# Output projection of a hybrid SSD/GLA layer split around the last GLA heads, and its opening stage reordered

## The chip, the cores and the metric

The kernel runs on one core of one Trainium2 chip. It is one program with five engines (TensorE or PE, VectorE or DVE, ScalarE or ACT, GpSimd or POOL, SyncE or SP), each of which takes its own instructions in order, and with DMA queues that engines issue to. The metric is the device time of one execution in microseconds; three runs are shown of the kernel before.

## What is computed

Two layers of a backbone over 256 latent tokens and 256 context tokens, `D_MODEL` = 1024, all in float32. Only layer 0 and its entry are touched here:

```python
mod = silu(c) @ ada_w[layer] + ada_b[layer]      # 6 x 1024: sh1, sc1, g1, sh2, sc2, g2
h = rmsnorm(x, norm1_w) * (1 + sc1) + sh1
z, xbc, dt, q, k, v, lr, r = split(h @ w_in)      # one input projection
xbc = silu(conv(xbc)); y = ssd_scan(...); o = gla_scan(...)
y = rmsnorm((y + d_skip * x) * silu(z), groups=4) * ssd_norm_w
o = rmsnorm(o, per head) * gla_norm_w * silu(r)
x = x + g1 * (concat([y, o]) @ w_out)             # w_out: 2048 x 1024
x = x + g2 * (relu(norm2(x) @ w1) ** 2 @ w2)      # MLP
```

Both token streams (256 each) have their own modulation vector. Layer 1 (HGRN2 and S5) follows with the same frame.

## The kernel before, in words

Activations that feed a matmul are held transposed, as 8 tiles of 128 features x 512 tokens. Every float32 product is made of three matmuls of a split type: `hhi`/`hlo` are the high and low part of the activations, `whi`/`wlo` those of a weight tile, and `mm3` (line 101) adds hi x hi, hi x lo and lo x hi. A weight tile is loaded by `wtile` (line 211) into one of four `wraw` buffers on SyncE's queue, ScalarE makes `whi` of it and VectorE `wlo`. An output tile of 128 features is 8 k-tiles x 3 = 24 matmuls of 512 columns into one of four PSUM tiles `psd`. Smaller products use four PSUM tiles `pss`.

`ada_steps` (line 227) makes 2048 columns of the modulation as a generator: eight k-steps (two loads of 512 KB into `wraw` buffers, four matmuls that the trace lists as eight records), then a copy, then transposes into `mod`: ten steps. `step(ad)` runs it on by one. Group (0,1) holds g1, which the output projection needs; group (0,2) holds sc2 and g2, for the MLP's norm and its end.

The opening (up to line 829) loads 512 token rows, scales them by their inverse norm, transposes them to `xh`, makes the first 2048 columns of the modulation from `araw` loads in three chunks of k-tiles (0 to 3, 4 and 5, 6 and 7), applies them to get `h`, and uses each chunk for the first four tiles of the input projection. The rows without norm are transposed to `xT` too, which is written to a DRAM buffer `xd` from GpSimd's queue and read back for the residual.

Then come convolutions, the SSD chunks, and the GLA heads in four steps `t_` of two heads. `gla_in(t_)` projects q and k and makes the scan's factors and states in a chain of small operations over ScalarE, VectorE and PE; `gla_out(t_)` makes attention and outputs. As cover, the loop runs generators between them: `fill` (the z projection, one group of 256 columns a step, and at the end the SSD norm) by `ZN[t_]` steps and `ad` by `ADN[t_]`. After the loop, the output projection runs in two parts: 8 transposes of `xtm` (the SSD half), 8 tiles; then the same for `vtm` (the GLA half), of which the last four tiles are done by token halves with the next norm between.

The program is traced in this order, and a scheduler that simulates the engines' times then sets the order on each engine, earlier traced instructions first among those that it takes to be ready. Buffers of one ring are handed out in the order of the trace.

Of the kernel before, what the change touches and what calls it, by code (L numbers as in the profile page):

```python
# [26 lines left out]
CB = 4  # L27
NALT = 100
NID = 8
DTM = 11  # L30
NF = 4
AR = 12
ZN = 3, 1, 2, 2
ADN = 0, 6, 11, 0
WA = 0, 1
QP = -2, 1, 2, 5
VP = -2, -1, 0, -1
GP = -1, 0, 4, 6
# [3 lines left out]
def emit(tc, A, out):  # L42
# [63 lines left out]
    def tr(o, i, rows=P):  # L106
        PE.transpose(o, i, ident[:rows, :rows])  # L107
# [646 lines left out]
    xn = tl(sp, [P, 4, DM], "xn")  # L754
    xh = tl(sp, [P, 8, T], "xh")
    ss = tl(sp, [P, 4], "ss")
    for b in range(2):
        for c in (2 * b, 2 * b + 1):
            S.activation(out=xn[:, c], in_=xt[:, c], func=AF.Square, accum_out=ss[:, c:c + 1])
        s2_ = ss[:, 2 * b:2 * b + 2]  # L760
        act(s2_, s2_, AF.Ln, scale=1.0 / DM, bias=eps)
        act(s2_, s2_, AF.Exp, scale=-0.5)
        for c in (2 * b, 2 * b + 1):
            ts(V, xn[:, c], xt[:, c], ss[:, c:c + 1], MUL)
    for k in range(8):
        ps = ps_s()
        for c in range(4):
            tr(ps[:, c * P:(c + 1) * P], xn[:, c, k * P:(k + 1) * P])
        if k % 2:
            V.tensor_copy(xh[:, k], ps)  # L770
        else:
            act(xh[:, k], ps, AF.Copy)
    h = tuple(tl(hp, [P, 8, T], n_, F32R) for n_ in ("hhi", "hlo"))
    scl = tl(cp, [P, 8, 2], "ms01")
    W0 = A["ssd_gla_w_in"][0]
    W1i = A["hgrn_s5_w_in"][0]
    order = (8, 9, 10, 11, 12, 13, 14, 15, 0, 1, 2, 3, 4, 5, 6, 7)
    first = {}
    for k0, nk in ((0, 4), (4, 2), (6, 2)):
        ps = ps_s()  # L780
        ks, n = slice(k0, k0 + nk), nk * P
        for kk in range(0, 8, 4 // nk):

            raw = tl(sp, [P, 4 // nk, 2, n], "araw", bufs=AR)
            for j in range(2):
                Q.dma_start(out=raw[:, :, j], in_=A["ada_w"][0, kk * P:(kk + 4 // nk) * P, j * DM + k0 * P:j * DM + k0 * P + n].rearrange(
                    "(k p) c -> p k c", p=P))
            for k in range(4 // nk):
                for g in range(4):
                    PE.matmul(ps[32 * g:32 * g + 32, :n // 2], lhsT=cs[:, kk + k],  # L790
                              rhs=raw[:, k, g // 2, n // 2 * (g % 2):n // 2 * (g % 2) + n // 2],
                              start=(kk + k == 0), stop=(kk + k == 7), skip_group_check=True, tile_position=(0, 32 * g))
        wq = [wtile(W0, kk, 2, 1024 + P * order[0], NF * P) for kk in range(k0, k0 + nk, 2)]
        if k0 == 0:
            small_t(ra, vA, P)
        sb = tl(sp, [P, 256], "adasb")
        act(sb[:, :n // 2], ps[:, :n // 2], AF.Copy)
        p2 = ps_s()
        nb = nk // 2
        for b in range(nb):  # L800
            tr(p2[:, b * P:(b + 1) * P], sb[:, b * P:(b + 1) * P])
        dst = mod[0][:, 0:16].rearrange("p (j k) s -> p j k s", j=2)[:, :, ks].rearrange("p j (h b) s -> p j h b s", h=2)
        src = p2[:, :nb * P].rearrange("p (b j h r) -> p j h b r", b=nb, j=2, h=2)[:, :, :, :, 0:2]
        bias = vA[:, 0:16].rearrange("p (j k) -> p j k", j=2)[:, :, ks].rearrange("p j (h b) -> p j h b", h=2)
        for s in range(2):
            for j in range(2):
                tt(V, dst[:, j, :, :, s], src[:, j, :, :, s], bias[:, j], ADD)
        mod_scale(scl, 0, 1, ks)
        for k in range(k0, k0 + nk):
            for s in (1, 0):  # L810
                sc_, sh_ = scl[:, k, s:s + 1], mod[0][:, k, s:s + 1]
                act(h[0][:, k, HALF[s]], xh[:, k, HALF[s]], AF.Identity, scale=sc_, bias=sh_)
                ts(V, xh[:, k, HALF[s]], xh[:, k, HALF[s]], sc_, MUL, sh_, ADD)
            tt(V, h[1][:, k], xh[:, k], h[0][:, k], SUB)
        for i, m in enumerate(order[:NF]):
            if k0 == 0:
                first[m] = ps_d()
            c_ = slice(P * i, P * i + P)
            for kk in range(k0, k0 + nk):
                w = [w_[:, kk % 2, c_] for w_ in wq[(kk - k0) // 2]]  # L820
                mm3(first[m], w, (h[0][:, kk], h[1][:, kk]), kk == 0, kk == 7)
        for k in range(k0, k0 + nk):
            ps = ps_s()
            for c in range(4):
                tr(ps[:, c * P:(c + 1) * P], xt[:, c, k * P:(k + 1) * P])
            act(xT[:, k], ps, AF.Copy)
    small_t(rb, vB, 104)
    small_t(rc, vC, P)
    st.close()
# [16 lines left out]
    def dt_proj():  # L846

        raw = tl(wp, [P, 8, P], "wraw", bufs=RAW)
        V.memset(raw, 0.0)
        for i, c0 in enumerate((3072, 3088, 5152, 5168)):  # L850
            Q.dma_start(out=raw[:, :, 32 * i:32 * i + 16], in_=W0[:, c0:c0 + 16].rearrange("(k p) c -> p k c", p=P))
        w = wsplit(raw, 8, P)
        ps = ps_d()
        gemm_f(ps, w, ktiles(h))
        act(dlr, ps, AF.Copy)
# [469 lines left out]
            lin_out(g2, pmask, units, put)  # L1325

    scr[0] = lambda: tl(g2, [P, T], "ge1", bufs=2)
    cur = gla_in(0, gla_w(0))
    wn = gla_w(1)
    for t_ in range(4):  # L1330
        step(fill, ZN[t_])
        nxt = gla_in(t_ + 1, wn) if t_ < 3 else None
        wn = gla_w(t_ + 2) if t_ < 2 else None
        step(ad, ADN[t_])
        if t_ == 3:
            drain(fill)
            step(ad, max(0, 10 - adn[0]))
        gla_out(t_, cur)
        cur = nxt
    gla.close()  # L1340


    lo_eng[:] = [V]
    WO = A["ssd_gla_w_out"][0]
    mgs = ExitStack()
    mg = pool("mixg", stack=mgs, side="right")
    scr[0] = lambda: tl(mg, [P, T], "adasb")
    for part, src in enumerate((xtm, vtm)):
        if part == 0:
            mx = [tl(hp, [P, 8, T], n, F32R) for n in ("hhi", "hlo")]  # L1350
        else:
            mx = [tl(mg, [P, 8, T], n, F32R) for n in ("mgh", "mgl")]
        for f in range(8):
            ps = ps_s()
            for c in range(4):
                tr(ps[:, c * P:(c + 1) * P], src[:, c, f * P:(f + 1) * P])
            nw = vB[:, 16 + f:17 + f] if part == 0 else vB[:, 96:97]
            act(mx[0][:, f], ps, AF.Copy, scale=nw)
            stt(V, mx[1][:, f], ps, nw, mx[0][:, f], MUL, SUB)
        if part == 0:  # L1360
            xT = tl(xp, [P, 8, T], "xtm")
            S.dma_start(out=xT, in_=xd.rearrange("k p t -> p k t"))
        def add_out(m):
            def put(s, ps):
                a = HALF[s]
                stt(V, xT[:, m, a], ps[:, a], mod[0][:, 16 + m, s:s + 1], xT[:, m, a], MUL, ADD)
            return put

        nf = 8 if part == 0 else 4
        for m in range(nf):  # L1370
            step(ad, WA[part])
            w = wtile(WO, 8 * part, 8, m * P, P)
            ps = ps_d()
            gemm_f(ps, w, ktiles(mx))
            for s in (1, 0):
                add_out(m)(s, ps)
# [346 lines left out]
```

## Time and profile before

| | |
|---|---|
| median of 3 runs | 1479.78 us (1475.62 to 1483.78) |
| the profiled execution | 1482.16 us, span 1480.4 us |
| PE busy | 1426.6 us, 96% |
| DVE, ACT, POOL busy | 942.2, 688.3, 303.0 us |
| mean granted clock of PE | 0.973 |
| HBM read, written | 206.39 MB, 14.46 MB |

An engine's busy time counts its instructions' spans, so a PE at half clock is as busy as at full clock; the granted clock has to be read beside it (1.00 is 2.4 GHz, 0.50 is 1.2 GHz). The page's slices show the clock at or near 9 (that is 0.9 or more) throughout, except for two slices of 8 and 5 some way into the span. The chain that ended last lies on PE for 78% of the span.

### The profile page before, as it was taken

Reading aid. Unit: us, or ns where it says so; the run is one execution under the profiler, and the core shown is the slowest. Engines: PE = TensorE matmul, PEld = TensorE weight load, DVE = VectorE, ACT = ScalarE, POOL = GpSimd, SP = SyncE. Lnnn points to the kernel's source line nnn. Section 1 sums busy time; section 2 is a strip of 40 time slices with the busy share of each in tenths; the row PEclk is TensorE's granted clock in tenths of the full one; section 3 lists DMA queues with packets and bytes.
Section 4 is the critical chain, followed back from the end, with each engine's and each line's share of the span. In section 5 each row is a group of like instructions: output and inputs, shape, how many; then the busy total and the mean of one; then the engine's idle time right before and its main releaser. Section 6 shows DMA issues by size and latency. Waiting matters only on the chain.

```text
span 1480.4 us, 24457 instructions
## 1 busy us (share of the span) xinstructions
PE 1426.6 (96%) x9662; PEld 1222.3 (83%) x9662; DVE 942.2 (64%) x1596; ACT 688.3 (46%) x1316; POOL 303.0 (20%) x340
## 2 busy tenths in 40 slices
PE   6999999999979999999999999999999999899998
PEld 4788998878746889877777777799988888899998
DVE  4698678876753455854563743374886988655543
ACT  5565545375532234531322422353286786555532
POOL 3000000000000003098077861122500000044210
PEclk9999999999985999999999999999999999999999
DMA  9733444421275433466467656649835332566762
GB/s 333 185 92 85 126 122 118 125 58 58 86 240 160 138 103 105 121 179 197 143 187 218 192 169 186 192 165 202 194 114 157 103 106 66 157 186 170 206 179 86
DMA packets 291151, 222.45 MB, mean 150 GB/s; under 512 B 22902, under 2 KB 270124, under 8 KB 291036
## 3 DMA queue, kind: packets, MB, share of 16 engines
q1 hardware_dynamic: 252752, 182.75, 42.5%
q0 software_dynamic: 6144, 22.05, 4.9%
q10 hardware_dynamic: 32140, 16.09, 4.4%
q8 instruction: 76, 1.25, 0.4%
q14 instruction: 39, 0.32, 0.1%
HBM read 206.39 MB, written 14.46 MB: 149 GB/s over the span
## 4 chain that ended last, share of the span: by engine, by line
PE 78%; DVE 8%; DMA 8%; ACT 4%; issue 2%; ACTq 0%; SPq 0%; DVEq 0%
PE psd L99 65%; PE pss L99 6%; DMA R<-acd 3%; PE pss L237 3%; PE pss L107 2%; DMA araw<-in_ada_w_dram 2%; DVE wlo L87 1%; DMA wraw<-in_ada_w_dram 1%; ACT hL L80 1%; DVE xtm L87 1%; ACT whi L80 1%; PE pss L652 1%; DMA U<-ud 0%; DMA ud<-s5r 0%; ACT R L80 0%
## 5 line engine op out<-in xcount | busy, mean ns | idle before, releaser
L87 DVE TENSOR_TENSOR wlo<-wraw,whi 128x1024 fp32r<-128x1024 f32 (+1 forms) x250 | 323.6, 1298 | 206.7 <-ACT whi L80 205.0
L80 ACT ACTIVATE whi<-wraw 128x1024 fp32r<-128x1024 f32 (+1 forms) x250 | 260.6, 1045 | 351.7 <-DMA wraw<-in_mlp_w_dram 170.7
L99 PE MATMUL psd<-hlo,whi 128*128 128x512 f32 (+1 forms) x1112 | 381.6, 345 | 1.3 <-DVE hlo L87 1.3
L99 PE MATMUL psd<-hhi,whi 128*128 128x512 f32 (+1 forms) x1112 | 378.5, 348 | 3.6 <-ACT hhi L80 3.6
L99 PE MATMUL psd<-hhi,wlo 128*128 128x512 f32 (+1 forms) x1112 | 380.8, 344 | 0.6 <-DVE wlo L87 0.6
L99 PEld LDWEIGHTS psd<-hhi,whi 128*128 128x128 f32 x1112 | 209.5, 191 | 36.0 <-ACT hhi L80 4.2
L99 PEld LDWEIGHTS psd<-hlo,whi 128*128 128x128 f32 x1112 | 211.3, 190 | 25.2 <-DVE hlo L87 2.3
L99 PEld LDWEIGHTS psd<-hhi,wlo 128*128 128x128 f32 x1112 | 211.3, 190 | 25.1 <-DVE wlo L87 1.0
L99 PE MATMUL psd<-wlo,hhi 128*128 128x256 f32 x576 | 165.5, 288 | 2.8 <-DVE wlo L87 2.8
L99 PE MATMUL psd<-whi,hlo 128*128 128x256 f32 x576 | 164.8, 286 | 0.0
L99 PE MATMUL psd<-whi,hhi 128*128 128x256 f32 x576 | 164.4, 287 | 0.0
L99 PEld LDWEIGHTS psd<-wlo,hhi 128*128 128x128 f32 x576 | 111.1, 193 | 4.7 <-DVE wlo L87 3.0
L99 PEld LDWEIGHTS psd<-whi,hhi 128*128 128x128 f32 x576 | 110.8, 193 | 2.7 <-issue 1.3
L99 PEld LDWEIGHTS psd<-whi,hlo 128*128 128x128 f32 x576 | 111.1, 193 | 0.6 <-issue 0.2
L99 PE MATMUL psd<-hidh,whi 128*128 128x512 f32 (+1 forms) x288 | 107.7, 375 | 0.0
L99 PE MATMUL psd<-hidl,whi 128*128 128x512 f32 (+1 forms) x288 | 105.6, 367 | 0.0
L99 PE MATMUL psd<-hidh,wlo 128*128 128x512 f32 (+1 forms) x288 | 105.5, 366 | 0.0
L87 POOL TENSOR_TENSOR nsa<-nsa,nsq 128x256 f32<-128x256 f32 x28 | 26.1, 934 | 370.1 <-ACT nsq L80 369.8
L96 DVE SCALAR_TENSOR_TENSOR xtm<-psd,mod,xtm 128x256 f32<-128x256 f32 x96 | 42.2, 476 | 66.6 <-PE psd L99 59.2
L99 PE MATMUL psd<-hl,whi 128*128 128x256 f32 x256 | 72.9, 285 | 0.0
L99 PE MATMUL psd<-hh,wlo 128*128 128x256 f32 x256 | 72.9, 285 | 0.0
L99 PE MATMUL psd<-hh,whi 128*128 128x256 f32 x256 | 72.4, 283 | 0.0
(448 smaller groups left out, 2447.4 us busy)
## 6 DMA issues: line engine op xcount, KB each, us to landing
wraw<-in_mlp_w_dram SPq DMA_DIRECT2D x128, 512.0 KB, 4.2
wraw<-in_ada_w_dram SPq DMA_DIRECT2D x80, 512.0 KB, 3.8
wraw<-in_ssd_gla_w_in_dram SPq DMA_DIRECT2D x48, 512.0 KB, 4.2
wraw<-in_hgrn_s_w_in_dram SPq DMA_DIRECT2D x43, 512.0 KB, 4.2
araw<-in_ada_w_dram SPq DMA_DIRECT2D x32, 256.0 KB, 7.8
R<-acd ACTq DMA_DIRECT2D x32, 256.0 KB, 3.9
wraw<-in_ssd_gla_w_out_dram SPq DMA_DIRECT2D x16, 512.0 KB, 4.6
wraw<-in_hgrn_s_w_out_dram SPq DMA_DIRECT2D x12, 384.0 KB, 3.4
```

Of the source, the lines that this page charges most:

```text
L80: ins = S.activation(out=out_, in_=in_, func=func, scale=scale, bias=bias)
L87: eng.tensor_tensor(out=o, in0=a, in1=b, op=op)
L96: eng.scalar_tensor_tensor(out=o, in0=a, scalar=s, in1=b, op0=op0, op1=op1)
L99: PE.matmul(o, lhsT=l, rhs=r, start=start, stop=stop, skip_group_check=True)
L107: PE.transpose(o, i, ident[:rows, :rows])
L237: ins = PE.matmul(ps[32 * gg:32 * gg + 32], lhsT=cs[:, k], rhs=raws[gg // 2][:, gg % 2 * T:gg % 2 * T + T], start=(k == 0), stop=(k == 7), ...
L652: PE.matmul(ps[64 * t2:64 * t2 + 64, 64 * a:64 * a + 64], lhsT=W1[i][:, a0 + a, 64 * t2:64 * t2 + 64], rhs=U[:, 2 * (a0 + a) + t2], start= ...
```

## The change

The output projection's loop is cut in two. A generator `ssd_out` holds the transposes of `xtm`, the load of `xT` and the eight tiles of the SSD half, with one step of `ad` ahead of each tile. The GLA loop runs it by `SN` = 0, 0, 5, 4 steps: five (the transposes and four tiles) behind `gla_out(2)` and four behind `gla_out(3)`. The GLA half stays behind the loop. `ADN` changes from 0, 6, 11, 0 to 0, 6, 4, 0, so group (0,1) is completed ahead of `gla_out(2)`, and the k-steps of (0,2) go with the tiles. `ZN` changes from 3, 1, 2, 2 to 2, 1, 1, 1, and what is left of `fill` (the last steps, with the norm) is run ahead of `gla_out(2)` instead of `gla_out(3)`.

In the opening, the 512 raw rows are transposed to `xT` right after they are loaded (VectorE copies them out of PSUM, ScalarE copies `xh`), the chain from the modulation's matmuls to `h` gets priority in the scheduler, and the first four tiles are fed k-tile by k-tile instead of tile by tile. The small dt projection is made after convolution tile 13 instead of 11, and its buffer is cleared by GpSimd instead of VectorE.

```diff
-DTM = 11
+DTM = 13
-ZN = 3, 1, 2, 2
-ADN = 0, 6, 11, 0
-WA = 0, 1
+ZN = 2, 1, 1, 1
+ADN = 0, 6, 4, 0
+SN = 0, 0, 5, 4
...
+    def turned(src, b, put):
+        for k in range(0, 8, 2):
+            ps = ps_s()
+            for i in range(4):
+                tr(ps[:, i * P:(i + 1) * P], src[:, 2 * b + i % 2, (k + i // 2) * P:(k + i // 2 + 1) * P])
+            put((slice(None), slice(k, k + 2), slice(256 * b, 256 * b + 256)), ps.rearrange("p (k t) -> p k t", k=2))
...
-    for k in range(8):
-        ps = ps_s()
-        for c in range(4):
-            tr(ps[:, c * P:(c + 1) * P], xn[:, c, k * P:(k + 1) * P])
-        if k % 2:
-            V.tensor_copy(xh[:, k], ps)
-        else:
-            act(xh[:, k], ps, AF.Copy)
+        turned(xt, b, lambda at, ps: V.tensor_copy(xT[at], ps))
+        turned(xn, b, lambda at, ps: act(xh[at], ps, AF.Copy))
...
+        with tc.high_priority():
             sb = tl(sp, [P, 256], "adasb")
...
-        for i, m in enumerate(order[:NF]):
-            if k0 == 0:
-                first[m] = ps_d()
-            c_ = slice(P * i, P * i + P)
-            for kk in range(k0, k0 + nk):
+        if k0 == 0:
+            first = {m: ps_d() for m in order[:NF]}
+        for kk in range(k0, k0 + nk):
+            for i, m in enumerate(order[:NF]):
...
                 mm3(first[m], w, (h[0][:, kk], h[1][:, kk]), kk == 0, kk == 7)
-        for k in range(k0, k0 + nk):
-            ps = ps_s()
-            for c in range(4):
-                tr(ps[:, c * P:(c + 1) * P], xt[:, c, k * P:(k + 1) * P])
-            act(xT[:, k], ps, AF.Copy)
...
-        V.memset(raw, 0.0)
+        G.memset(raw, 0.0)
...
+    def out_tile(mx, part, m):
+        w = wtile(WO, 8 * part, 8, m * P, P)
+        ps = ps_d()
+        gemm_f(ps, w, ktiles(mx))
+        for s in (1, 0):
+            add_out(m)(s, ps)
+
+    def ssd_out():
+        mx = [tl(hp, [P, 8, T], n, F32R) for n in ("hhi", "hlo")]
+        turned_mix(mx, xtm, 0)
+        res["x"] = tl(xp, [P, 8, T], "xtm")
+        S.dma_start(out=res["x"], in_=xd.rearrange("k p t -> p k t"))
+        yield
+        for m in range(8):
+            step(ad)
+            out_tile(mx, 0, m)
+            yield
...
+    so = ssd_out()
     for t_ in range(4):
         step(fill, ZN[t_])
         nxt = gla_in(t_ + 1, wn) if t_ < 3 else None
         wn = gla_w(t_ + 2) if t_ < 2 else None
         step(ad, ADN[t_])
-        if t_ == 3:
+        if t_ == 2:
             drain(fill)
-            step(ad, max(0, 10 - adn[0]))
+            step(ad, 10 - adn[0])
         gla_out(t_, cur)
+        step(so, SN[t_])
         cur = nxt
     gla.close()
```

`turned_mix` holds the eight groups of transposes with their scaling into `hhi`/`hlo`, as they stood in the loop before.

## Rows read from the trace of the kernel before

**Rows 1.** Stretches: length, busy us (instructions) by engine, granted clock, DMA share, GB/s.
```profile
0.00:31.70 31.70, 17.12 (x168) 12.37 (x168) 13.12 (x34) 16.44 (x34) 12.43 (x28) 1.00 0.96 322
300.00:310.00 10.00, 7.21 (x48) 7.00 (x48) 9.42 (x13) 8.40 (x20) 0.00 (x0) 0.83 0.03 5
398.60:440.00 41.40, 31.97 (x278) 16.71 (x279) 25.94 (x45) 16.25 (x51) 0.00 (x0) 0.92 0.73 246
440.00:486.00 46.00, 46.00 (x205) 29.38 (x206) 17.85 (x26) 10.43 (x42) 0.00 (x0) 0.51 0.55 168
745.00:830.00 85.00, 85.00 (x443) 62.97 (x443) 44.33 (x44) 23.45 (x31) 67.62 (x55) 1.00 0.69 200
```

**Rows 2.** Waits of PE, 398.6 to 486 us: total, times, longest.
```profile
PE pss L237 <- DMA wraw<-in_ada_w_dram: 8.2, 5, 3.2
```

**Rows 3.** Timeline of PE, 400 to 452 us: start, length, instructions, idle before.
```profile
400.49 0.97 PE L99 MATMUL pss<-g0qt,g0kt 64*64 64x128 f32 x15
...
402.95 1.06 PE L99 MATMUL pss<-g0qt,g0kt 64*64 64x128 f32 x16 [0.25 <-DVE pm L1193]
405.01 1.06 PE L237 MATMUL pss<-wraw,cs 128*32 128x512 f32 x8 [1.01 <-DMA wraw<-in_ada_w_dram]
406.01 1.09 PE L99 MATMUL pss<-g1qt,g1kt 64*64 64x64 f32 x16
...
410.81 1.06 PE L237 MATMUL pss<-wraw,cs 128*32 128x512 f32 x8
...
422.53 1.06 PE L237 MATMUL pss<-wraw,cs 128*32 128x512 f32 x8 [3.20 <-DMA wraw<-in_ada_w_dram]
...
426.66 1.93 PE L237 MATMUL pss<-wraw,cs 128*32 128x512 f32 x8 [2.23 <-DMA wraw<-in_ada_w_dram]
...
451.69 1.97 PE L99 MATMUL pss<-g0qt,g0kt 64*64 64x128 f32 x16
```

**Rows 4.** Timeline of SyncE's queue, 355 to 560 us.
```profile
370.38 88.87 SPq L233 DMA_DIRECT2D wraw<-in_ada_w_dram  x28
```

**Rows 5.** The chain that ended last: start, length, what, how many.
```profile
290.18 6.95 PE psd L99 x58
...
512.86 20.89 PE psd L99 x92
```

**Rows 6.** DMA issues, 396 to 486 us: count, size, median us to landing.
```profile
wraw<-in_ada_w_dram SPq DMA_DIRECT2D x26, 512.0 KB, 5.3
wraw<-in_ssd_gla_w_out_dram SPq DMA_DIRECT2D x8, 512.0 KB, 4.2
```

**Rows 7.** DMA issues, 745 to 830 us (MLP of layer 0).
```profile
wraw<-in_mlp_w_dram SPq DMA_DIRECT2D x14, 512.0 KB, 5.5
wraw<-in_ada_w_dram SPq DMA_DIRECT2D x12, 512.0 KB, 3.6
```

**Rows 8.** Timeline of PE, opening.
```profile
30.63 1.17 PE L790 MATMUL pss<-araw,cs 128*32 128x128 f32 x16 [0.33 <-DMA araw<-in_ada_w_dram]
31.72 1.19 PE L99 MATMUL psd<-hhi,whi 128*128 128x512 f32 x4
...
51.19 1.94 PE L790 MATMUL pss<-araw,cs 128*32 128x128 f32 x58
...
53.66 1.04 PE L107 MATMUL pss<-ident,xt 128*128 128x128 f32 x8
...
56.41 1.20 PE L99 MATMUL psd<-hhi,whi 128*128 128x512 f32 x4 [1.51 <-ACT hhi L80]
```

**Rows 9.** Timeline of ScalarE, opening.
```profile
26.77 2.06 ACT L80 ACTIVATE xT<-pss 128x512 f32<-128x512 f32 x4
28.69 4.04 ACT L80 ACTIVATE hhi<-xh,mod,ms 128x256 fp32r<-128x256 f32 x8
```

**Rows 10.** Timeline of GpSimd: first and last of the four writes of `xT`.
```profile
28.15 0.77 POOL L887 DMA_DIRECT2D xd<-xT  x1 [12.69 <-ACT xT L80]
...
57.63 0.71 POOL L887 DMA_DIRECT2D xd<-xT  x1 [17.40 <-DMA wraw<-in_ssd_gla_w_in_dram]
```

More of the change, by code (lines that the diff above doesn't have):

```diff
@@ L777, in emit @@
     order = (8, 9, 10, 11, 12, 13, 14, 15, 0, 1, 2, 3, 4, 5, 6, 7)
-    first = {}
     for k0, nk in ((0, 4), (4, 2), (6, 2)):
@@ L795, in emit @@
             small_t(ra, vA, P)
[L796 to L808, printed above, removed]
-        for k in range(k0, k0 + nk):
[L810 to L814, printed above, removed]
@@ L815, in emit @@
-        for i, m in enumerate(order[:NF]):
-            if k0 == 0:
-                first[m] = ps_d()
-            c_ = slice(P * i, P * i + P)
-            for kk in range(k0, k0 + nk):
-                w = [w_[:, kk % 2, c_] for w_ in wq[(kk - k0) // 2]]
-                mm3(first[m], w, (h[0][:, kk], h[1][:, kk]), kk == 0, kk == 7)
-        for k in range(k0, k0 + nk):
-            ps = ps_s()
-            for c in range(4):
-                tr(ps[:, c * P:(c + 1) * P], xt[:, c, k * P:(k + 1) * P])
-            act(xT[:, k], ps, AF.Copy)
+        with tc.high_priority():
+            sb = tl(sp, [P, 256], "adasb")
+            act(sb[:, :n // 2], ps[:, :n // 2], AF.Copy)
+            p2 = ps_s()
+            nb = nk // 2
+            for b in range(nb):
+                tr(p2[:, b * P:(b + 1) * P], sb[:, b * P:(b + 1) * P])
+            dst = mod[0][:, 0:16].rearrange("p (j k) s -> p j k s", j=2)[:, :, ks].rearrange("p j (h b) s -> p j h b s", h=2)
+            src = p2[:, :nb * P].rearrange("p (b j h r) -> p j h b r", b=nb, j=2, h=2)[:, :, :, :, 0:2]
+            bias = vA[:, 0:16].rearrange("p (j k) -> p j k", j=2)[:, :, ks].rearrange("p j (h b) -> p j h b", h=2)
+            for s in range(2):
+                for j in range(2):
+                    tt(V, dst[:, j, :, :, s], src[:, j, :, :, s], bias[:, j], ADD)
+            mod_scale(scl, 0, 1, ks)
+            for k in range(k0, k0 + nk):
+                for s in (1, 0):
+                    sc_, sh_ = scl[:, k, s:s + 1], mod[0][:, k, s:s + 1]
+                    act(h[0][:, k, HALF[s]], xh[:, k, HALF[s]], AF.Identity, scale=sc_, bias=sh_)
+                    ts(V, xh[:, k, HALF[s]], xh[:, k, HALF[s]], sc_, MUL, sh_, ADD)
+                tt(V, h[1][:, k], xh[:, k], h[0][:, k], SUB)
@@ L827, in emit @@
+        if k0 == 0:
+            first = {m: ps_d() for m in order[:NF]}
+        for kk in range(k0, k0 + nk):
+            for i, m in enumerate(order[:NF]):
+                w = [w_[:, kk % 2, P * i:P * i + P] for w_ in wq[(kk - k0) // 2]]
+                mm3(first[m], w, (h[0][:, kk], h[1][:, kk]), kk == 0, kk == 7)
     small_t(rb, vB, 104)
@@ L1327, in emit, with turned_mix @@
     scr[0] = lambda: tl(g2, [P, T], "ge1", bufs=2)
[L1328 to L1334, printed above, removed]
-        if t_ == 3:
-            drain(fill)
-            step(ad, max(0, 10 - adn[0]))
[L1338 to L1343, printed above, removed]
-    WO = A["ssd_gla_w_out"][0]
[L1345 to L1352, printed above, removed]
+    WO = A["ssd_gla_w_out"][0]
+    res = {}
+    def turned_mix(mx, src, part):
         for f in range(8):
@@ L1359, in emit, with add_out, put @@
             stt(V, mx[1][:, f], ps, nw, mx[0][:, f], MUL, SUB)
[L1360 to L1376, printed above, removed]
+    def add_out(m):
+        def put(s, ps):
+            a = HALF[s]
+            x_ = res["x"][:, m, a]
+            stt(V, x_, ps[:, a], mod[0][:, 16 + m, s:s + 1], x_, MUL, ADD)
+        return put
+    def out_tile(mx, part, m):
+        w = wtile(WO, 8 * part, 8, m * P, P)
+        ps = ps_d()
+        gemm_f(ps, w, ktiles(mx))
+        for s in (1, 0):
+            add_out(m)(s, ps)
[9 more added lines that the diff above has]
+            yield
+    cur = gla_in(0, gla_w(0))
+    wn = gla_w(1)
+    so = ssd_out()
+    for t_ in range(4):
+        step(fill, ZN[t_])
+        nxt = gla_in(t_ + 1, wn) if t_ < 3 else None
+        wn = gla_w(t_ + 2) if t_ < 2 else None
+        step(ad, ADN[t_])
+        if t_ == 2:
+            drain(fill)
+            step(ad, 10 - adn[0])
+        gla_out(t_, cur)
+        step(so, SN[t_])
+        cur = nxt
+    gla.close()
+    lo_eng[:] = [V]
+    mgs = ExitStack()
+    mg = pool("mixg", stack=mgs, side="right")
+    scr[0] = lambda: tl(mg, [P, T], "adasb")
+    mx = [tl(mg, [P, 8, T], n, F32R) for n in ("mgh", "mgl")]
+    turned_mix(mx, vtm, 1)
+    xT = res["x"]
+    for m in range(4):
+        step(ad)
+        out_tile(mx, 1, m)
     drain(ad)
```

## The prediction

> **What bounds the kernel now.** I read the page first: TensorE (PE) is busy for 96% of the span, so only time in which it waits, or in which it runs at its lower clock, can be won. The table of stretches says where that is [rows 1]. From 398.6 to 440.0 us PE is busy for 31.97 of 41.4 us. From 440.0 to 486.0 us it is busy all the time, but at a granted clock of 0.51, which is the 1.2 GHz level instead of 2.4: 22.5 of these 46 us are lost although no idle time shows. Outside this stretch only short holes are left, as the 2.8 us of 300 to 310 us.
>
> The list of waits says what PE waited for there: the loads of `ada_w`, 8.2 us in five waits [rows 2]. The timeline shows the mechanism [rows 3]. PE runs the small matmuls of `gla_out` and, between them, one k-step of `ada_steps` after another (eight records, 1.06 us at full clock). It takes its instructions in order, so a k-step whose two loads have not landed stops all of it: 1.01 us at 405.01, 3.20 at 422.53, 2.23 at 426.66. After these holes the clock is down, and the attention block that took 1.06 us at 402.95 takes 1.97 at 451.69. The queue of SyncE shows the cause of the holes: from 370.38 us it needs 88.87 us for 28 loads, 3.17 us each, through the four `wraw` buffers [rows 4]. Dense work is not there to stand in between: the tiles of the output projection come after all of it, and their eighth ends at 512.86 + 20.89 = 533.8 us in the chain that ended last [rows 5].
>
> **The late stretch, from the eighth k-step on.** The steps of (0,1) are finished at 426.66 + 1.93 = 428.6 us [rows 3], and the change keeps all eight of them ahead of `gla_out(2)`. From there to 533.8 us the kernel now takes 105.2 us. The same work after the change, at full clock:
> - 8 tiles of the SSD half x 24 matmuls x 0.227 us (20.89 us for 92 [rows 5]) = 43.6 us.
> - 8 k-steps x 1.06 us = 8.5 us. Now seven of them stand in this stretch and the last behind it, so 1.1 us comes back later.
> - `gla_out(2)` and `gla_out(3)`, two heads each. One pair at full clock: the attention blocks from 400.49 to 402.95 less a wait of 0.25 (2.2 us), then 1.06 and 1.09; the first head's outputs from there to 410.81 (3.7), and as much for the second: 11.75 us [rows 3]. Two pairs: 23.5 us.
> - 32 transposes of `xtm` at 0.13 us (eight `xt` transposes of the same form take 1.04 us [rows 8]) = 4.1 us.
>
> Sum 79.7 us, so 25.5 us less, and with the k-step behind it 26.6. What remains of the loss must be taken off. Loads: 24 of them in 79.7 us is one per 3.32 us. The MLP of layer 0 ran 26 in 85 us, 3.27 us each, with PE busy throughout at full clock [rows 1, 7], so this pace is carried; I charge 2 us for the uneven mixture (two loads for a k-step, one for a tile), between 0 and the pace at which all is serial (rival 4). Clock: the dense tiles stand between the two pairs of heads, but an isolated pair may still run low; I charge 4 us, between 0 and 23.5 (both pairs at 1.2 GHz). That leaves -20.6 us.
>
> **Before 428.6 us.** The fourth group of z moves from ahead of `gla_in(2)` to behind it: 96 matmuls at 0.12 us (6.95 us for 58 [rows 5]) = 11.5 us of dense work that can now stand in the 6.4 us of waits between 405 and 427 [rows 3]. Its two weight loads queue behind twelve `ada_w` loads in SyncE's queue, so it may itself come late. I take half, -3.2 us (0 to -6.4). In return `t_` = 0 has one group of z less as cover, where 2.8 us of hole are today [rows 1]: 0, at worst +2.8. Norm, transposes of `xtm`, and their scaling on ScalarE and VectorE now fall among the chains of heads 4 to 7, but both engines are busy for less than two thirds there (25.94 and 16.25 of 41.4 us [rows 1]). The load of `xT` from `xd` moves ahead by some 60 us on ScalarE's queue, where it can hold up what is behind it only until the last of the 32 transposes is done; the 4 us above cover that. Dropping one accumulation order for another in `first` changes no count of matmuls.
>
> **The opening.** PE reaches its first projection matmul at 31.72 us, behind `ada_w` matmuls that waited for their load (0.33 us at 30.63). From there to the end of the first four tiles it is in work except for gaps of the small chain: the last `araw` matmul ends at 53.13 and the next projection matmul starts at 56.41, 3.3 us, in which eight `xt` transposes are the filler [rows 8]. The change takes the `xt` transposes to the first 20 us, when PE is waiting anyway: two groups of eight stand behind 31.72 today, but one of them only fills that gap, so 0.8 us. The chain gets priority: ScalarE's one `xT` copy in that gap goes, 0.6 us. At the start, ScalarE runs four `xT` copies (2.06 us) before the first `hhi` at 28.69 [rows 9], and VectorE's memset of the dt weights goes to GpSimd; of these 2.06 us I take 0.6, because the first matmul also stands behind that load. Sum -2.0, at best -3.5. The dt weights, issued after the m = 13 tile instead of m = 11, are wanted only by the dt stage behind all convolutions, so moving them is taken as 0.
>
> Against it: `xT` is complete some 10 us earlier, and GpSimd, idle then, writes it to `xd` at once. The four writes of 512 KB are issued from 28.15 to 57.63 us today [rows 10]. The DMA engines are full all that time: share 0.96, 322 GB/s [rows 1]. All 2.1 MB ahead of the loads of chunk two would cost them 2.1 MB / 322 GB/s = 6.5 us, and 3.3 if half of them fall ahead of those loads already today. I take 0 for the forecast, since PE has 48 matmuls (10.9 us) of the first chunk to do, and leave the rest to rival 1.
>
> **Sum.** -20.6 - 3.2 - 2.0 = -25.8 us. The profiled execution took 1482.16 us (span 1480.4); 1456.4 after. The median of the runs shown is 1479.78, 2.4 below the profiled one, so 1454 us.
>
> **The rivals.**
> 1. *The xd write displaces the opening loads* (17%). PE's order has `araw` matmuls ahead of the first projection matmul, so it waits 3.3 to 6.5 us, 4.9 in the middle; less the 1.4 still saved, the opening is +3.5 instead of -2.0: 1459.5 us. For it speaks that the first matmul stands behind a load already [rows 8]; against it, that the writes start at 28.15 us today, ahead of that matmul too [rows 10]. The Trainium skill, "DMA: Bandwidth & Descriptors", section "Queues, rings and completion order", says that each DMA engine takes turns between the queues that have work, so GpSimd's write would not wait behind SyncE's loads but take every other turn. By that rule this rival is right, in its upper half; no row of before shows the turn itself.
> 2. *The clock stays low through both pairs of heads* (12%). If the tiles end up behind the heads in PE's order, the pairs cost 23.5 us more instead of 4: 1473.5 us. For it: PE was busy without a gap from 440 to 486 us and still at 0.51. Against: from 400.49 to 410.81 us the same kind of work ran at full clock [rows 3].
> 3. *The order does not change in effect* (8%). A scheduler places the instructions by its own estimate of time; if it leaves the tiles behind `gla_out(3)`, only the opening is won: 1478 us.
> 4. *The loads go serial and it gets slower* (7%). If a tile's load cannot run ahead of the k-step before it in the four buffers, a tile takes 5.3 (`ada_w` landing) + 1.06 + 4.2 (tile landing) [rows 6] + 5.45 = 16.0 us even without its casts; eight take 128.1 instead of the 105.2 of now, 22.9 more, less 1.1 for the last k-step and 2.0 of the opening: 1499.5 us. It decides from 13.2 us per tile. Against it stands the pace of the MLP [rows 7].
>
> **How the numbers follow.** The forecast holds 56%. Its own range is 1443 (all waits and clock won, the best opening: -6.4 - 26.6 - 3.5 = -36.5) to 1464 (nothing won before 428.6 us, 2.8 lost at `t_` = 0, loads and clock each 2 dearer). With rivals 1 and most of 2 the range is 1443 to 1474; above it lie rivals 3, 4 and the rest of 2. A difference of 0.5%, 7.4 us, is about what a measurement of this kernel can tell. Rival 2 falls on its edge (1472.4). Faster: forecast, rival 1 and 5% of rival 2's 12, 0.78. Within 0.5%: rival 3 and the other 7%, 0.15. Slower: 0.07.
>
> **What would show it.** The granted clock between 440 and 486 us near 1; k-steps of 1.06 us with tiles between them; `xtm` transposes before `gla_out(3)`; the eighth SSD tile near 510 us; waits for `ada_w` under 4 us in all; the first projection matmul near 31 us and none of the `xt` transposes after it. A clock still at 0.5 there, or a wait for `wraw` at each tile, would make the number wrong.

## The result, and the profile after

The changed kernel is slower: 1492.03 us in the median of 11 runs (1484.24 to 1495.19), the kernel before 1477.62 in 11 runs (1460.64 to 1487.61); ratio 1.012, 95% interval 1.0083 to 1.0156. The forecast was 1454 us. Ratios here are taken over undisturbed runs alone, so they can differ from the quotient of two medians, by 0.6% at most. The profiled execution is the slowest of the 11 (1495.19 us), with a span of 1493.5 us (1480.4 before).

Where the time goes shows first in the chain that ended last (start, length, what, how many). The piece that began at 290.18 us before [rows 5] begins earlier now; the first 48 matmuls of the MLP, at 631.93 us before, come later:
```profile
286.92 6.95 PE psd L99 x58
...
415.09 23.40 PE psd L99 x144
...
520.63 4.30 DMA wraw<-in_ssd_gla_w_out_dram
...
527.78 5.27 DMA wraw<-in_ssd_gla_w_out_dram
...
645.16 11.11 PE psd L99 x48
```
At 287 us the kernel is 3.3 us ahead, at 645 us 13.2 us behind: 16.5 us are lost in the GLA heads and the output projection, and nothing after them. The stretches of [rows 1], with 310 to 398.6 and 486 to 533.8 us added (busy us and instructions by engine, granted clock, DMA share, GB/s):
```profile
0.00:31.70 31.70, 15.87 (x132) 10.74 (x132) 12.27 (x35) 14.55 (x31) 13.53 (x30) 0.93 0.95 334
310.00:398.60 88.60, 80.03 (x557) 62.15 (x554) 56.72 (x89) 45.78 (x124) 0.00 (x0) 0.83 0.23 73
398.60:440.00 41.40, 41.40 (x210) 27.96 (x208) 19.71 (x27) 19.39 (x56) 0.00 (x0) 0.78 0.30 102
440.00:486.00 46.00, 40.27 (x251) 30.28 (x249) 24.39 (x39) 13.17 (x40) 0.00 (x0) 0.70 0.33 108
486.00:533.80 47.80, 46.79 (x237) 33.50 (x240) 18.87 (x29) 10.43 (x28) 0.00 (x0) 0.89 0.57 183
```
The stretch that the change was aimed at, 440 to 486 us, did get a higher clock (0.70 for 0.51). But 310 to 398.6 us, where the kernel before was busy for 88.17 of 88.6 us at a clock of 1.00, now has 8.6 us of holes and a clock of 0.83. The list of waits of PE from 290 to 610 us (total, times, longest) names the holes:
```profile
PE pss L107 <- DVE ke L87: 6.2, 2, 5.3
PE pss L107 <- DVE su L96: 3.1, 1, 3.1
PE pss L237 <- DMA wraw<-in_ada_w_dram: 2.3, 1, 2.3
PE pss L99 <- DVE su L96: 2.3, 1, 2.3
```
The waits for `ada_w` fell from 8.2 us [rows 2] to 2.3. In their place PE waits for VectorE: for the keys `ke` and the states `su`, which are the chain of small operations in `gla_in`. The timeline of PE at the first of these holes:
```profile
362.87 2.08 PE L99 MATMUL pss<-dlr,gw 16*128 16x512 f32 x4
...
370.07 0.79 PE L99 MATMUL pss<-vtm,pa 128*128 128x128 f32 x2
376.16 0.90 PE L107 MATMUL pss<-ident,ke 128*128 128x128 f32 x3 [5.30 <-DVE ke L87]
377.97 0.90 PE L107 MATMUL pss<-ident,ke 128*128 128x128 f32 x3 [0.90 <-DVE ke L87]
...
389.63 1.75 PE L99 MATMUL pss<-g0qt,g0kt 64*64 64x128 f32 x15
```
The `gw` matmuls start pair 2's chain at 362.87 us, and its keys can be transposed from 376.16: 13 us. PE has the rest of `gla_out(0)` to do, until 370.86, then nothing. Half clock doesn't begin with this hole, though. The `gw` matmuls take 2.08 us here and 1.13 before, and two stretches show that the clock fell 8.8 us ahead of the hole, behind the small matmuls of `gla_out(0)`, with hardly a gap (columns as above):
```profile
354.50:362.00 7.50, 7.46 (x88) 6.03 (x88) 5.71 (x10) 1.00 (x2) 0.00 (x0) 1.00 0.00 0
362.00:370.80 8.80, 8.80 (x26) 5.36 (x25) 6.17 (x9) 4.77 (x16) 0.00 (x0) 0.50 0.00 0
```
The kernel before has z's fourth group, 96 matmuls from 346.9 to 372.4 us, between these outputs, and runs them at full clock.

The last line of the timeline is pair 1's second attention block: its 15 records take 1.75 us, where 16 took 1.06 us at 402.95 before [rows 3]; that is half clock. In the kernel before the same place, on its timeline, has a hole of no more than 0.23 us, and 48 projection matmuls of pair 3 (384.5 to 395.7 us) stand between:
```profile
383.47 1.13 PE L99 MATMUL pss<-dlr,gw 16*128 16x512 f32 x4
...
395.55 0.49 PE L107 MATMUL pss<-ident,ke 128*128 128x128 f32 x3
396.26 0.55 PE L107 MATMUL pss<-ident,ke 128*128 128x128 f32 x3 [0.23 <-DVE ke L87]
```
After the change these 48 and z's fourth group come only at 415.09, as one block of 23.40 us (the `x144` in the chain above). SyncE's queue shows why z's group is late (start, length, issues):
```profile
325.15 76.40 SPq L233 DMA_DIRECT2D wraw<-in_ada_w_dram  x12
405.33 0.93 SPq L214 DMA_DIRECT2D wraw<-in_ssd_gla_w_in_dram  x2
```
Its two loads stand behind twelve `ada_w` loads, whose buffers come free only as PE reaches the k-steps. Pair 3's own weights are not late: ScalarE has no weight cast between 341.98 and 412.28 us, so they were cast before, and their matmuls start at 415.62 without a wait. They come late because the order on PE has them behind the first of z's.

In the opening, rival 1 shows as it was described. GpSimd issues its four writes together, PE waits 5.78 us, and the first projection matmul comes at 33.90 us (31.72 in [rows 8]):
```profile
17.56 2.91 POOL L883 DMA_DIRECT2D xd<-xT  x4 [1.46 <-DVE xT L773]
```
```profile
32.23 1.74 PE L791 MATMUL pss<-araw,cs 128*32 128x128 f32 x16 [5.78 <-DMA araw<-in_ada_w_dram]
33.90 2.08 PE L99 MATMUL psd<-hhi,whi 128*128 128x512 f32 x4
```
By 287 us the kernel is ahead all the same.

### The profile page after: what moved, and what is told of

Read it like the earlier page. It is cut to its first block, busy times and chain, and to the rows that moved or that the text cites. A ratio compares the mean times of both kernels' runs of the same rounds, so it can differ in the third digit from the quotient of the medians.

```text
span 1493.5 us, 24439 instructions
## 1 busy us (share of the span) xinstructions
PE 1434.7 (96%) x9662; PEld 1223.6 (82%) x9662; DVE 942.0 (63%) x1599; ACT 684.9 (46%) x1312; POOL 301.6 (20%) x341
## 4 chain that ended last, share of the span: by engine, by line
PE 75%; DMA 10%; DVE 8%; ACT 4%; issue 2%; ACTq 0%; SPq 0%; DVEq 0%
PE psd L99 63%; PE pss L99 7%; DMA R<-acd 3%; PE pss L237 2%; DMA wraw<-in_ssd_gla_w_out_dram 2%; DMA araw<-in_ada_w_dram 2%; PE pss L107 2%; DVE wlo L87 2%; ACT whi L80 1%; DMA wraw<-in_mlp_w_dram 1%; ACT hL L80 1%; DMA xtm<-xd 1%; DMA U<-ud 1%; DMA ud<-s5r 0%; DVE su L96 0%
```

## The experiments

All are compared with the kernel before on the same chip, 1474.8 to 1479.2 us in the median by batch; a variant has 6 runs, or 12 (cover_all, cover_old_opening, cover_xd_late, cover_gates). Five batches lie behind the table, so medians of variants from different batches can differ by some us for that alone. For each, the last two columns add up windows of 2.5 us from 290 to 610 us of one profiled execution: holes are 2.5 us less PE's busy time, clock loss is busy time x (1 - granted clock).

| kernel | median us | ratio to before, 95% interval | holes us | clock loss us |
|---|---|---|---|---|
| before | 1477.6 | | 12.7 | 27.9 |
| the change | 1492.0 | 1.0083 to 1.0156 | 16.6 | 39.9 |
| opening_only | 1499.9 | 1.0108 to 1.0220 | 19.1 | 46.3 |
| late_only | 1492.6 | 1.0051 to 1.0157 | 15.5 | 36.6 |
| z_early | 1499.8 | 1.0104 to 1.0221 | 20.1 | 37.5 |
| xd_late | 1492.7 | 1.0055 to 1.0167 | 16.8 | 30.2 |
| dense_fill | 1501.3 | 1.0135 to 1.0265 | 22.6 | 18.7 |
| no_split | 1498.9 | 1.0129 to 1.0239 | 23.1 | 40.4 |
| mixed_a | 1496.8 | 1.0116 to 1.0220 | 24.3 | 27.9 |
| gate_late | 1493.8 | 1.0097 to 1.0201 | 20.9 | 38.6 |
| cover_old_end | 1497.9 | 1.0107 to 1.0225 | 10.7 | 49.5 |
| cover_split | 1491.7 | 1.0076 to 1.0182 | 12.1 | 42.4 |
| cover_mix | 1487.7 | 1.0050 to 1.0158 | 11.2 | 35.5 |
| cover_all | 1475.4 | 0.9976 to 1.0044 | 13.7 | 15.1 |
| cover_no_split | 1493.8 | 1.0073 to 1.0190 | 17.4 | 31.6 |
| cover_old_opening | 1475.6 | 1.0026 to 1.0099 | 9.2 | 24.6 |
| cover_xd_late | 1468.5 | 0.9928 to 1.0015 | 8.2 | 15.9 |
| cover_gates | 1483.6 | 1.0042 to 1.0128 | 12.3 | 23.6 |

**Which half of the change?** The first theory (Q) was the queue: twelve `ada_w` loads ahead of z's. Rivals: the opening (O), or the split itself (S).

opening_only: the new opening with the old end.
```diff
-ZN = 2, 1, 1, 1
-ADN = 0, 6, 4, 0
-SN = 0, 0, 5, 4
+ZN = 3, 1, 2, 2
+ADN = 0, 6, 11, 0
+WA = 0, 1
...
```


> The kernel before with the opening of the changed kernel alone (xT made early, priority for the chain, k-tile by k-tile, dt projection after tile 13, memset on GpSimd); the GLA loop and the output projection as before. Theory Q (the loss lies in the order of loads in the GLA loop): 1 to 3 us slower than before, because the xd write delays the second chunk's loads and about half of that is made up behind it. Rival S (the split itself costs): the same. Rival O (the opening is the loss): 12 to 15 us slower than before, as the whole change.

late_only: the old opening with the new end.
```diff
-DTM = 13
+DTM = 11
...
```


> The changed kernel with the opening of before; ZN, ADN, SN and the split projection as changed. Q and S: 11 to 15 us slower than before, nearly the whole change. O: within 3 us of before. In the trace Q wants PE at half clock from about 360 to 415 us with no dense work, z's fourth group and gla_in(3) behind the twelve ada_w loads.

z_early: z's fourth group is traced, and so loaded, ahead of the gate steps.
```diff
-ZN = 2, 1, 1, 1
+ZN = 3, 1, 1, 1
```


> The changed kernel with ZN = 3, 1, 1, 1 in place of 2, 1, 1, 1: the fourth group of z, and its two loads, come ahead of the twelve ada_w loads of t_ = 1 again; all else as changed. Q: the dense work of z and gla_in(3) (23 us) fills the chains again, 14 to 20 us faster than the changed kernel, 1472 to 1478 us. S: it stays within 4 us of the changed kernel. O: the same.

xd_late: the four writes held behind GpSimd's memset.
```diff
-            G.dma_start(out=xd.rearrange("k p t -> p k t")[:, k:k + 2], in_=xT[:, k:k + 2])
+            behind(G.dma_start(out=xd.rearrange("k p t -> p k t")[:, k:k + 2], in_=xT[:, k:k + 2]), late[0])
```


> The changed kernel with the four writes of xT to xd held behind GpSimd's memset of the dt weights (41 us in the changed kernel), so that none of them shares the DMA engines with the first weight loads. If the writes at 17.56 us are what made the weights land at 28.48 us instead of 24.03, the first projection matmul comes 2 to 4 us earlier; Q and S: the whole is 2 to 4 us faster than the changed kernel, no more. O: 12 us faster.

Q fell: z_early has z's loads ahead of the gate steps and is no faster than the change. O fell as the only cause, since late_only is slow with the old opening. But opening_only, at +20 us, is further off than any theory had it. With the new opening and the old, unsplit end the kernel reaches its first `gw` matmul at 291.51 us, 5.5 us before the kernel before (297.05), and still ends 20 us behind. Its late program is traced word for word as before, but the scheduler orders it otherwise. On its timeline the second half of pair 2's `gw` comes behind the projection matmuls instead of ahead of them, and nothing is left beside the chain:
```profile
383.66 1.34 PE L99 MATMUL pss<-dlr,gw 16*128 16x512 f32 x2
...
389.88 1.12 PE L99 MATMUL pss<-dlr,gw 16*128 16x512 f32 x2
394.20 0.49 PE L107 MATMUL pss<-ident,ke 128*128 128x128 f32 x3
400.42 0.90 PE L107 MATMUL pss<-ident,ke 128*128 128x128 f32 x3 [5.73 <-DVE ke L87]
```
xd_late does start its projections at 28.99 us instead of 33.90, but its first `gw` matmul is at 294.71 (293.80 in the change): the writes in the opening cost nothing by then. Its lower clock loss (30.2 us) lies in the heads, as in the stretch from 440 to 486 us, at 0.79 there instead of 0.70; its median is the change's all the same.

**Is it the clock?** Theory C: the lost time is clock, which dense matmuls would hold.

dense_fill: three matmuls that nothing reads behind each output sum of pairs 0 to 2, 72 in all.
```diff
             mm(os_, pa[:, i], u_[2], not inter, True)
+            if HOT[0]:
+                ps = ps_d()
+                for _ in range(HOT[0]):
+                    behind(PE.matmul(ps, lhsT=h[0][:, 0, :P], rhs=h[0][:, 1], start=True, stop=True,
+                                     skip_group_check=True), LASTMM[0])
```


> This kernel is the changed one with extra work that nothing uses: three 512-column matmuls behind each of the 24 output sums of GLA pairs 0 to 2, 72 in all, 16.3 us of TensorE at the 0.227 us that one takes at the full clock. Theory C: the 16.5 us that the changed kernel loses between 290 and 645 us are clock: once a hole has brought the granted clock to 0.5, the small matmuls of the GLA outputs and the gate steps run on at 0.5 without a pause, and only long runs of 512-column matmuls raise it. By windows of 2.5 us from 290 to 610 us, the changed kernel lost 39.9 us to the clock and 16.6 us to holes, the kernel before 27.9 and 12.7. So dense work between the outputs should hold the clock, the loss should fall from 40 to 15 to 25 us, and the added 16 us come back: 1478 to 1492 us, with the outputs of pairs 1 and 2 at a granted clock of 0.8 or more. Rival S (the waits of the split and of its rings are the loss, the clock only follows): the dummies are 16 to 30 us of extra work, 1508 to 1522 us.

no_split:
```diff
-SN = 0, 0, 5, 4
+SN = 0, 0, 0, 9
```


> The changed kernel with all eight SSD tiles behind the last GLA pair instead of between pairs 2 and 3; the order up to 440 us is unchanged. Theory C: what is lost before 440 us stays lost (10 us of the 16.5), and the outputs of pairs 2 and 3 both run at half clock: 1488 to 1500 us. Rival S (the split between the pairs is what costs): back at the time of before, 1474 to 1482 us.

mixed_a:
```diff
-ZN = 2, 1, 1, 1
-ADN = 0, 6, 4, 0
-SN = 0, 0, 5, 4
+ZN = 3, 1, 1, 1
+ADN = 5, 5, 0, 0
+SN = 0, 0, 2, 4
...
             step(ad, 10 - adn[0])
+            step(so, 3)
         gla_out(t_, cur)
```


> The changed kernel with the ten gate steps moved into the first two GLA pairs (five each), z's groups 3, 1, 1, 1, and the transposes and two SSD tiles ahead of the outputs of pair 2, so that the instruction order has the outputs of pairs 2 and 3 in pieces between 24-matmul tiles. Theory C: the last 60 us of the stretch run at the full clock instead of 0.5 to 0.9, worth 12 to 20 us: 1472 to 1482 us. Rival S: more of the split and of its loads between the heads, so 1492 to 1505 us.

gate_late:
```diff
-ADN = 0, 6, 4, 0
+ADN = 0, 0, 10, 0
```


> The changed kernel with no gate steps ahead of z's third group: the ten come in a block behind the outputs of pair 1, so the loads of z's group and of the last GLA pair's projections are no longer behind twelve gate loads, and these 96 dense matmuls stand in pieces between the outputs of pair 1. Theory C: 360 to 415 us at the full clock, worth 10 to 15 us, against a block of eight gate steps that waits for its loads (at 5.3 us each, less what runs ahead in the ring), 5 to 15 us: 1482 to 1494 us. Rival S: no gain from the clock, and the block's wait on top: 1500 to 1510 us.

dense_fill and mixed_a came out slower than C had put them (mixed_a in S's range), no_split and gate_late at the upper end of C's ranges. In dense_fill the clock still did what C says. The stretches 398.6 to 533.8 us of dense_fill:
```profile
398.60:440.00 41.40, 40.19 (x256) 28.71 (x253) 21.08 (x30) 15.23 (x45) 0.00 (x0) 0.92 0.51 174
440.00:486.00 46.00, 39.04 (x268) 28.36 (x267) 26.96 (x42) 17.84 (x51) 0.00 (x0) 0.93 0.20 60
486.00:533.80 47.80, 46.65 (x259) 32.13 (x257) 19.18 (x30) 8.97 (x26) 0.00 (x0) 0.89 0.61 196
```
The clock is 0.92 and 0.93 where the change has 0.78 and 0.70, and the clock loss falls by 21.2 us (39.9 to 18.7), more than the 16.3 us of added matmuls. But the waits for `ke` rose, from 6.2 us to 14.7, the longest 10.2, and all holes by 6.0 us, which took the gain back (16.3 - 21.2 + 6.0 = 1.1). The span is 6.8 us longer; 2.2 of that stood already at the first `gw` matmul (296.0 and 293.8 us), and the rest is not explained. mixed_a waits for `ke` for 17.3 us in all, gate_late for `ada_w` for 12.1. So there are two costs that go together: a hole where a pair's chain has no dense work beside it, and half clock in small work that has no dense work between. The half clock is not just a consequence of the hole, since in the change the clock fell ahead of it. no_split was as slow as the split kernels: against S.

**Putting the cover back.** Theory D: each pair's chain needs about 48 dense matmuls beside it. The projections of a pair are put behind the `gw` matmuls of the pair before (`mm` puts each matmul behind those in `hold[0]`, for order alone). Rival N: the kernel before is a chance best.

cover_old_end is opening_only with this for pair 3 alone:
```diff
+            hold[0] = gates[2] if t_ == 3 else ()
             gemm_f(ps, w, ktiles(h))
+            hold[0] = ()
...
-            mm(ps, gw[b0:b0 + 16, t_ * P:(t_ + 1) * P], dlr[b0:b0 + 16])
+            gates[t_].append(mm(ps, gw[b0:b0 + 16, t_ * P:(t_ + 1) * P], dlr[b0:b0 + 16]))
```


> The opening of the changed kernel with the old, unsplit end (as in the run opening_only), and one thing more: the 48 query and key projection matmuls of GLA pair 3 are held behind the gate matmuls of pair 2, where they stand in the kernel before. Theory D: what costs is cover. From a pair's gate matmuls to the transposes of its keys ScalarE and VectorE need 12 to 13 us, and in every kernel slower than before TensorE had 6 us or less to do in that time for pair 2 (a hole of 5 to 6 us on the keys), after which the small matmuls ran at half clock; in the kernel before 48 dense matmuls (11 us) stand there. By D this run is 15 to 30 us faster than opening_only (1499.9): 1470 to 1485 us, with no wait of over 1 us for the keys of pair 2. Rival N (the kernel before is a chance best, the opening's other order costs by itself): 1494 to 1502 us.

cover_split is z_early with it for all pairs:
```diff
+            hold[0] = gates[t_ - 1] if t_ else ()
```


> The changed kernel with z's groups as 3, 1, 1, 1 (as in z_early, 1499.8 us) and each pair's projections held behind the gate matmuls of the pair before, so that pair 2's element chain has pair 3's 48 projection matmuls beside it. Theory D: 10 to 20 us faster than z_early: 1480 to 1490 us. Rival S (the split costs): 1494 to 1502 us, while cover_old_end comes back to before.

cover_mix adds tiles ahead of `gla_out(2)`:
```diff
-SN = 0, 0, 5, 4
+SN = 0, 0, 2, 4
...
+            step(so, 3)
         gla_out(t_, cur)
```


> As cover_split, and the transposes with the first two SSD tiles are put ahead of the outputs of pair 2 in priority, so that tiles stand between the outputs of pairs 2 and 3 instead of behind those of pair 2. Theory D: outputs of pairs 2 and 3 at the full clock, another 8 to 15 us: 1468 to 1480 us. Rival S: slower than cover_split, 1496 to 1508 us, as more loads stand between the heads.

cover_all (besides, `ZN` is the change's again) holds z's fourth group behind the `gw` matmuls of pair 3:
```diff
-ADN = 0, 6, 4, 0
+ADN = 0, 4, 6, 0
...
-        step(fill, ZN[t_])
+        if t_ != 2:
+            step(fill, ZN[t_])
         nxt = gla_in(t_ + 1, wn) if t_ < 3 else None
+        if t_ == 2:
+            hold[0] = gates[3]
+            step(fill, ZN[t_])
+            hold[0] = ()
```


> As cover_mix, but z's groups as 2, 1, 1, 1 with the last one held behind the gate matmuls of pair 3, and the gate steps as 0, 4, 6, 0: each of the chains of pairs 1, 2 and 3 has about 48 dense matmuls beside it. Theory D: no wait of over 1 us for keys, the clock loss of 290 to 610 us from 40 us to under 20: 1460 to 1475 us, faster than both kernels. Rival S: 1494 to 1508 us.

cover_old_end has no wait for `ke` any more, and 10.7 us of holes in place of 19.1, but only 2 us of time came back: a wait of 2.14 us for `pm` now falls among the small matmuls of `gla_out(0)` at 373.51 us, the clock goes down there, and the loss by clock is the largest of all, 49.5 us. So the hole at the keys alone was not it (gate_late is slow too, with no wait for `ke` above 2.7 us): D in this narrow form missed, and the time, 1497.9 us, lies in N's range. cover_split, just outside D's range, is 8 us faster than z_early, and cover_mix, 8 us outside it, 4 us faster than cover_split. cover_all, with three edits to cover_mix that weren't taken apart (`ZN`, `ADN` and the hold on z's fourth group), then took 12 more. Its stretches:
```profile
310.00:398.60 88.60, 82.76 (x609) 63.99 (x612) 62.21 (x97) 50.24 (x139) 0.00 (x0) 0.99 0.29 92
398.60:440.00 41.40, 34.67 (x202) 24.15 (x195) 22.88 (x35) 19.13 (x55) 0.00 (x0) 0.77 0.34 112
440.00:486.00 46.00, 44.84 (x254) 30.84 (x253) 20.52 (x32) 9.33 (x28) 0.00 (x0) 0.85 0.57 175
486.00:533.80 47.80, 47.79 (x274) 34.95 (x273) 24.84 (x36) 15.85 (x35) 0.00 (x0) 1.00 0.63 181
```
From 486 us on, tiles and heads in turn, PE is never idle and never below the full clock. At pair 2 on its timeline, 46 dense matmuls now stand between these lines, and no wait:
```profile
361.21 1.13 PE L100 MATMUL pss<-dlr,gw 16*128 16x512 f32 x4
...
376.05 0.49 PE L111 MATMUL pss<-ident,ke 128*128 128x128 f32 x3
376.84 0.49 PE L111 MATMUL pss<-ident,ke 128*128 128x128 f32 x3
```
N falls: another order than that of before is as fast.

**What is the split worth, and the opening?** Four variants of cover_all.

cover_no_split:
```diff
-SN = 0, 0, 2, 4
+SN = 0, 0, 0, 9
...
-            step(so, 3)
```


> As cover_all (1475.4 us), but all eight SSD tiles behind the last GLA pair. Order theory with the split of use: the outputs of pairs 2 and 3 have no tiles between them and fall to half clock again, 8 to 15 us: 1483 to 1491 us. Order theory with the split worth nothing (dense cover of the three chains is all): 1473 to 1478 us. Split costs by itself: 1465 to 1472 us.

cover_old_opening, with the opening of the kernel before:
```diff
-DTM = 13
+DTM = 11
...
```


> As cover_all, with the opening of the kernel before. If the new opening is a wash, as the first GLA gate matmul says (293.8 us after, 297.1 before, so 3 us for it at most): 1475 to 1480 us. If the new opening costs (the x copy's writes at 17.6 us in the way of the first loads): 1466 to 1472 us. The rival that the opening was the loss would need 10 us or more: 1465 us or less.

cover_xd_late, with the edit of xd_late.

> As cover_all, with the four writes of the x copy held behind GpSimd's memset (as in xd_late), so that they don't stand among the opening's loads. If these writes are what the opening loses: 2 to 4 us faster than cover_all, 1471 to 1474 us; if they are hidden: 1474 to 1478 us.

cover_gates:
```diff
-ADN = 0, 4, 6, 0
+ADN = 1, 3, 6, 0
```


> As cover_all, with the ten gate steps as 1, 3, 6, 0 over the pairs instead of 0, 4, 6, 0, which puts the first four of them a pair earlier in the instruction order, ahead of the outputs of pair 0. If the waits for their loads (8.5 us in cover_all) and the clock that falls behind the longest (3.7 us at 398 us) are what is left: 5 to 10 us faster, 1465 to 1471 us, clear of the kernel before. If not, 1473 to 1480 us.

The split, in this order, is worth up to 18 us: 1493.8 us without it, 1475.4 with it, in different batches; the spans differ by 14.8 us. Some of this lies ahead of the tiles, as this edit too changes the order there: from the first `gw` matmul to the end of the eighth k-step the kernel without the split takes 140.5 us, cover_all 136.6. From 440 to 486 us the kernel without it is busy for 45.32 us at a clock of 0.65, against 0.85 above:
```profile
440.00:486.00 46.00, 45.32 (x245) 34.39 (x243) 23.96 (x38) 11.65 (x49) 0.00 (x0) 0.65 0.13 39
```
So S is not only unsupported but reversed. The old opening changes nothing that these runs can tell (1475.6; the two intervals overlap). cover_xd_late is the fastest of all, 1468.5 us. It is not clear of the kernel before (interval 0.9928 to 1.0015), whose runs in that batch went from 1455.8 to 1483.8 us, but its median is 23.6 us below the change's. Its reason isn't the one expected: its projections start 4.9 us sooner than in cover_all (28.49 and 33.37 us), yet its first `gw` matmul is later (297.58 and 293.96). It gains in the heads, where the waits for `ada_w` are 3.7 us instead of 8.5. cover_gates missed: with the gate steps earlier, VectorE comes late with the SSD norm, and PE waits for it once, for long:
```profile
442.60 4.00 PE L111 MATMUL pss<-ident,xtm 128*128 128x128 f32 x16 [7.34 <-DVE xtm L88]
```

## Why the prediction was wrong

Two steps failed. By its terms the eighth k-step ends at 428.6 - 3.2 - 2.0 = 423.4 us; it ended at 440.3, 16.9 us later. From there to the eighth tile it allows 79.7 + 2 + 4 = 85.7 us; that took 108.8, 23.1 us more. Together they make 40.0 us; the profiled execution (1495.2 us) missed its forecast of 1456.4 by 38.8.

**The step before 428.6 us (-3.2 us).** It took the moved z group only as filler for the waits on `ada_w`, and the cover taken away ahead of it at "0, at worst +2.8". What it didn't look for was what those dense matmuls already kept away. Z's group stood between the outputs of pair 0, and pair 3's projections filled the 13 us of pair 2's element chain; the list of waits of before showed nothing there for just that reason. With both gone to 415 us, 8.6 us of holes opened from 310 to 398.6 us, and the clock there fell from 1.00 to 0.83, which by that window's 80.03 us of busy time is 13.6 us. The step had seen that two loads stand behind twelve, but z_early shows that these loads alone are not the cause.

**The late stretch (-20.6 us).** In the change it won nothing: 108.8 us, with one k-step more than the 105.2 of before. The same stretch of the change and then of cover_all, from the end of the eighth k-step to that of the eighth tile:
```profile
440.30:549.10 108.80, 101.51 (x557) 74.07 (x554) 49.67 (x77) 29.21 (x75) 0.00 (x0) 0.83 0.48 150
430.50:526.50 96.00, 91.41 (x513) 63.79 (x510) 45.26 (x66) 25.50 (x69) 0.00 (x0) 0.89 0.54 165
```
By the first line the change lost 17.3 us to the clock there (4 charged) and 7.3 to holes, of which 5.4 are waits for `su`. What is left, 84.2 us, is work; the sum had 79.7 and left out pair 3's keys and states and the transposes of `ge` and `vtm`. The first tile came at 470 us, behind `gla_out(2)`; the `xtm` transposes did run ahead of `gla_out(3)` (463.0 to 477.2 us). The load of `xT` stands on the chain that ended last (9.93 us from 477.56), but PE's own wait behind it, for `pa`, is 0.9 us. In cover_all's order the mechanism works, and the stretch takes 96.0 us, still 10.3 more than the sum and its charges.

The other terms, the rivals and the signs:

- **The clock (4 us charged, 0 to 23.5).** The change loses 39.9 us to it from 290 to 610 us, more than before (27.9). The bound counted pairs 2 and 3 alone; the outputs of pair 0 (from 362 us) and pair 1, mostly at full clock before, now ran at half too.
- **Loads (2 us).** More than enough. From 440.3 us to the eighth tile the list of waits has 0.4 us for a cast of a tile's weight and none for `ada_w`, and from 519.5 us k-steps with a tile between follow each other on PE at 6.7 to 7.4 us, where the work is 6.5 and, in the last two, some transposes of `vtm`. Rival 4's 13.2 us didn't occur.
- **The opening (-2.0 us).** Rival 1 was right about the writes: they wait for nothing, and the first matmul came 2.2 us later than before instead of sooner. It was wrong about what they cost: at 287 us the kernel is 3.3 us ahead. That this is near the forecast -2.0 is no proof of its working, as the first matmul was to come sooner and didn't; late_only and cover_old_opening, with the old opening, also reach their first `gw` matmul at 294.5 us (293.8 in the change, 297.1 before). The DMA list of 10 to 70 us gives the writes 9.7 us to land (6.0 before). The Trainium skill, "DMA: Bandwidth & Descriptors", section "Queues, rings and completion order", has the engines take turns between queues. The first cast of a weight, at 28.48 us instead of 24.03, is in line with that; no row shows the turns.
- **Rival 2** came true in part: `gla_out(2)` stood ahead of the tiles in one piece at half clock, 449 to 470 us. Its 23.5 us were the price of pairs 2 and 3 alone.
- **"What would show it"** answered: `ada_w` waits under 4 us (2.3) and no `xt` transposes behind 31 us held; the clock from 440 to 486 (0.70, not near 1), the eighth tile and the first matmul (33.90, not 31) failed.
- **Not in the prediction at all:** that an edit to the opening reorders the heads 350 us later. The scheduler orders by its own estimate of time, and opening_only lost 20 us in code that it doesn't touch.

Over the 17 kernels of the table that do the kernel's own work alone, the span goes with holes plus clock loss: a straight line of 0.75 us of span per us lost fits one profiled execution of each within 3.8 us. Three things stay open: why one order of the scheduler bunches the small matmuls and another doesn't, which of cover_all's edits its last 12 us are owed to, and how much of cover_xd_late's lead over cover_all would stay in another order.

## What to carry to other kernels

Before dense work is moved, look for the waits that are not in the list because it hides them: follow each latency chain (here 13 us from a gate matmul to its keys) and note which matmuls stand beside it. Count time lost to the granted clock next to idle time, since a PE that is 100% busy at 0.5 looks full. Where a scheduler places instructions by its own estimate, compare the order of the whole program after any edit, not only near the edit, and pin the few dependencies that matter.

## What the hardware showed that was not expected

A full engine can fall to the low clock and stay there. In the kernel before, PE has no idle time from 440 to 486 us and stays at 0.51 [rows 1]; in the change, the small matmuls from 390 to 410 us run at half clock without a gap. Nor does a fall need a hole. The change's first, at 362 us, comes behind 7.46 us of small matmuls in 7.50 us, as its stretches above show, and late_only, xd_late and no_split fall at the same place in the same way, at 362.6 to 364.4 us. Other falls stand behind a hole: the one at 423.5 us in the kernel before behind 3.20 us [rows 3], that of cover_old_end behind 2.14. But small matmuls don't always bring a fall: from 396.8 to 419.3 us the kernel before runs them at 1.00, with 1.4 us of holes. What makes the difference stays open.

The clock came back behind runs of 512-column matmuls: from 415.09 us in the change (1.00 from 420 to 440), and in dense_fill, with three of them behind each output sum, two stretches stand at 0.92 and 0.93. The Trainium skill, "TensorE: Matmul & The Clock Gate", section "HAM oscillation — how this bites in real kernels", puts such losses down to idle gaps while TensorE waits for loads. The fall at 423.5 us, behind a wait for `ada_w`, agrees with it; the fall at 362 us without a gap, and the 46 us at 0.51 with no idle time, are not what it describes, and there the measurement decides.
